# Gated MLP: products accumulated in PSUM chains that ScalarE seeds, two plain pairs a layer, and the first pair's weight blocks made in attention

## The chip, the core and the metric

The kernel runs on one core of one Trainium2 chip. The metric is the device time of one execution in microseconds (us). Engines: TensorE (PE), VectorE (DVE), ScalarE (ACT), GpSimd (POOL) and SyncE (SP), which issues most loads.

## The reference, cut to what matters

A two-layer causal decoder trunk on 512 tokens with 1024 channels, all in float32. Each layer ends with a cross-attention and a gated MLP; the change lies in these two.

```python
def conv_ffn(x, norm, w_up, dw_w, dw_b, w_down):      # d_ff = 3072
    h = rms_norm(x, norm) @ w_up
    g = causal_dwconv(h[..., :D_FF], dw_w, dw_b)       # width 3
    u = h[..., D_FF:]
    return (jax.nn.gelu(g) * u) @ w_down

for layer in range(2):
    x = x + (mixer_ab(x) if layer == 0 else conformer_conv(x))
    x = x + cross_attn(x, mem, ...)                    # 4 heads, 256 memory tokens
    x = x + conv_ffn(x, ...)
return rms_norm(x, final_norm)
```

## The kernel before

Channels lie on the 128 partitions, tokens along the free dimension: an activation is 8 tiles of 128 x 512. Each operand of a matmul is a pair of rounded numbers, `hi` (made by ScalarE as a converting copy) and `lo` (made by VectorE as the difference); one product of a weight block and an activation block takes three matmuls (`mm3`: hi·hi, hi·lo, lo·hi; lines L186, L187, L188).

**Pairs.** The 3072 hidden channels are 24 groups `c` of 128. Each `c` has a gate block and a value block of w_up, together a "pair". The first `PLAIN` = 3 pairs are computed plainly: 8 k-blocks times 3 matmuls of 512 columns for the gate, the same for the value. The other 21 go through a two-by-two scheme with seven half products in place of eight (`Seven`, `Blocks`, `unit`): the weights of a pair are four 512-column blocks, from which sums r, z are formed; the seven left operands are named a11, a12, a22, s1, s2, s3, s4. Right operands are the halves of the normalised input (B11, B21, B22) and four sums of them (T1 to T4, made by `Seven.sums`, once for each k of 0 to 3). Each half product is 12 matmuls of 256 columns.

**Blocks of a pair.** The pair comes in by three loads (`Blocks.load`: r and z; `load_second`: a12 and a22). Each block needs a `high` (ScalarE, L797) and a `low` (VectorE, L804). The sums are formed in place by DMAs that add (GpSimd's queue), each issued behind a `low`: r += z after a11, z += a22 after a22, r += a22 after s3, r += a12 after s2. So s3 is made of r after the first addition, s1 of z after its addition.

**A unit of before** (`unit(c)`) makes the seven products in seven PSUM banks in turn, in the order a11, a12, s2, s3, s1, s4, a22. VectorE adds them together (`add`, L171), ScalarE copies the first home. `gating` then multiplies with the norm's factor `norm.r`, runs the convolution (Identity on ScalarE, two steps on VectorE), gelu (ScalarE), and makes `ys[c]`. Blocks of the next two pairs are converted in between. From c = 4 on, a unit also makes two down outputs of 12 matmuls of 512 columns (`Down.out`, tag `aux`), which VectorE adds to the residual `X` (`Down.sum`).

**Opening.** `opening()` makes the plain pairs (`start(0)` to `start(5)`, gates and values by turns) while the norm's factor is found from the sum of squares (`mean_of`, `scale_of`: a table load, a square root, a reciprocal L308) and while the last of the sums, `seven.sums(3)`, the first pair's blocks and the second pair's first blocks are made. `gate(c)` is the gate's path up to gelu, `values(c)` multiplies and makes the high part, `close(c)` the low part.

**Attention** runs before it: `scores` (products, row maximum L501 to L505, exponentials L510 and normalisation L517 on ScalarE), `transpose` (L531 on TensorE), `turned`, `mixed`, and `back`, the output projection that adds to `X` (L555) and feeds the MLP's norm.

**Order.** Both stages are under `manual_schedule`: on PE, ACT, DVE and POOL the instructions stand in the order in which the code is written, and an engine that waits holds up everything behind. SP's loads wait for a free buffer (the ring `raw` has 3, `wa` has 4).

Of the kernel before, what the change touches and what calls it, by code (L numbers as in the profile page):

```python
# [13 lines left out]
ALU = mybir.AluOpType  # L14
# [13 lines left out]
PLAIN = 3  # L28
# [33 lines left out]
def trunk(ctx: ExitStack, tc: tile.TileContext, I: dict, out: list):  # L62
# [121 lines left out]
    def mm3(ps, w, x, first, last):  # L184
        (wh, wl), (xh, xl) = w, x
        PE.matmul(ps, wh, xh, start=first, stop=False)  # L186
        PE.matmul(ps, wh, xl, start=False, stop=False)  # L187
        PE.matmul(ps, wl, xh, start=False, stop=last)  # L188
# [281 lines left out]
    def attention(layer, norm, mem, nxt, six):  # L470
# [197 lines left out]
        with tc.manual_schedule(engines=ORDERED):  # L668
# [25 lines left out]
            end(3, "a12")  # L694
        back(0, range(4))
# [18 lines left out]
    class Seven:  # L714
# [38 lines left out]
        def product(self, ps, w, j, first=True):  # L753
            for c in range(4):
# [6 lines left out]
                mm3(ps, blk(w, c * P), x, first and c == 0, c == 3)  # L761
# [55 lines left out]
    def ffn(layer, norm, nxt, seven):  # L817
        ys = {}

        class Down:  # L820
# [8 lines left out]
            def out(self, i, ps):  # L829
                for k in range(GC):  # L830
                    mm3(ps, blk(self.w, k * 2 * P + i * P), ys[self.g * GC + k], k == 0, k == GC - 1)
                return lambda: self.sum(i, ps)
# [7 lines left out]
        pairs = {c: Blocks(I["wpair"][layer * (CF - PLAIN) + c - PLAIN]) for c in range(PLAIN, CF)}  # L840
        downs = {c: Down(*divmod(c - GC, GC)) for c in range(GC, CF + GC)}

        early = set()

        def high(c, name):
            if c in pairs and (c, name) not in early:
                pairs[c].high(name)

        def low(c, name):
            if c in pairs and (c, name) not in early:  # L850
                pairs[c].low(name)

        def gating(c, f, g, ps, u3):
# [3 lines left out]
            V.tensor_tensor(g, g, norm.r, op=ALU.mult)  # L857
            A.activation(y, g, AF.Identity, scale=dw(2), bias=col("f_dw_b", layer * CF + c))
            yield
            add(f[:, :M], ps, u3)  # L860
            V.tensor_tensor(f, f, norm.r, op=ALU.mult)
            for s in (1, 2):
                V.scalar_tensor_tensor(y[:, s:], g[:, : T - s], dw(2 - s), y[:, s:], op0=ALU.mult, op1=ALU.add)
            yield
            A.activation(y, y, AF.Gelu_apprx_tanh)
            yield
            V.scalar_tensor_tensor(y, f, -1.0, y, op0=ALU.mult, op1=ALU.mult)
            ys[c] = act_r(), act_r()
# [3 lines left out]

        def unit(c):

# [989 lines left out]
```

## Time and profile before

| | |
|---|---|
| median of 3 runs | 1430.1 us (1429.94 to 1431.17) |
| span of the profiled execution | 1429.2 us |
| the profiled execution's time | not listed apart; its span lies 0.9 us below the median of the runs |
| PE busy | 1418.0 us (99%) |
| DVE busy | 1184.4 us (83%) |
| ACT busy | 800.7 us (56%) |
| POOL busy | 311.2 us (22%) |

The span falls into stages (from the timeline, us): mixer of layer 0 to about 245, attention to 355, the MLP's opening to 388, its 21 units to 709, the last down outputs to 731, the conformer to about 888, attention and MLP of layer 1 from about 935 to 1396, the final norm to the end. A row of a timeline is: start, duration, engine, line, operation, output<-inputs, partitions x elements, count, and in brackets the idle time just ahead with the engine whose work ended it. Matmul rows overlap by pipelining, so the price of a matmul is the distance of starts, not the duration shown.

### The profile page before, as it was taken

The numbers are of one execution on the slowest core, as the hardware profiler recorded it, in microseconds if no ns is written. First come the engines' busy times: TensorE is split into PE (matmuls) and PEld (weight loads), VectorE is DVE, ScalarE is ACT, GpSimd is POOL, SyncE is SP. The second block draws the span as 40 slices with busy tenths as digits, with TensorE's granted clock in tenths as the row PEclk, the third lists the DMA queues.
The fourth block names the chain that finished last, engine by engine and source line by source line (L and its number), as shares of the span: only waits on it lengthen the run. The fifth ranks groups of instructions, "written<-read, shape, count | busy, mean of one in ns | idle before, by whom it ended". The sixth has DMA issues, their size and how long they took to land.

```text
span 1429.2 us, 22885 instructions
## 1 busy us (share of the span) xinstructions
PE 1418.0 (99%) x8578; PEld 1259.4 (88%) x8578; DVE 1184.4 (83%) x1980; ACT 800.7 (56%) x1336; POOL 311.2 (22%) x325
## 2 busy tenths in 40 slices
PE   9999999999999999999999999999999999999998
PEld 7988888998899999999988777899889999999997
DVE  6987776778888888888888997978788988888885
ACT  7678754666644444544555547767665444444434
POOL 0011310200122221222008992010012222221201
PEclk9999999999999999999999999999999999999999
DMA  8523232542577777777432454345247876877741
GB/s 302 197 74 104 89 119 80 118 111 89 136 183 169 172 181 165 164 176 169 140 119 89 118 158 153 105 87 148 86 114 162 178 184 157 171 183 159 164 127 60
DMA packets 78591, 202.23 MB, mean 141 GB/s; under 512 B 8848, under 2 KB 9360, under 8 KB 78480
## 3 DMA queue, kind: packets, MB, share of 16 engines
q1 hardware_dynamic: 50544, 150.15, 33.6%
q0 software_dynamic: 27648, 50.34, 21.3%
q8 instruction: 67, 1.10, 0.3%
q14 instruction: 44, 0.36, 0.1%
q10 hardware_dynamic: 288, 0.27, 0.1%
HBM read 145.16 MB, written 2.10 MB: 103 GB/s over the span
## 4 chain that ended last, share of the span: by engine, by line
PE 90%; DVE 3%; DMA 2%; POOL 2%; issue 1%; ACT 1%; SPq 0%; POOLq 0%; DVEq 0%; ACTq 0%
PE mm L187 22%; PE mm L186 22%; PE mm L188 22%; PE aux L186 7%; PE aux L187 7%; PE aux L188 7%; PE mm L458 2%; DMA raw<-in_wv 1%; DVE wlo L167 1%; POOL actf L1469 1%; ACT whi L166 1%; PE aux L531 0%; POOL act L167 0%; POOL tmp L1290 0%; DMA raw<-in_pw 0%
## 5 line engine op out<-in xcount | busy, mean ns | idle before, releaser
L187 PE MATMUL mm<-act,whi 128*128 128x512 f32 (+2 forms) x1077 | 377.1, 350 | 0.6 <-DVE act L181 0.5
L188 PE MATMUL mm<-act,wlo 128*128 128x512 f32 (+2 forms) x1077 | 376.7, 350 | 0.0
L186 PE MATMUL mm<-act,whi 128*128 128x512 f32 (+2 forms) x1077 | 376.6, 351 | 0.0
L187 PEld LDWEIGHTS mm<-act,whi 128*128 128x128 f32 x1077 | 203.7, 189 | 29.0 <-DVE act L167 1.0
L186 PEld LDWEIGHTS mm<-act,whi 128*128 128x128 f32 x1077 | 203.4, 189 | 28.4 <-ACT tmp L1468 0.8
L188 PEld LDWEIGHTS mm<-act,wlo 128*128 128x128 f32 x1077 | 203.6, 189 | 25.8
L797 ACT ACTIVATE bigr<-raw 128x512 fp32r<-128x512 f32 x168 | 105.6, 628 | 166.8 <-DMA raw<-wa 70.4
L188 PE MATMUL mm<-bigr,bigr 128*128 128x256 f32 x672 | 190.2, 283 | 0.0
L187 PE MATMUL mm<-bigr,bigr 128*128 128x256 f32 x672 | 190.2, 283 | 0.0
L186 PE MATMUL mm<-bigr,bigr 128*128 128x256 f32 x672 | 190.0, 283 | 0.0
L171 DVE TENSOR_TENSOR tmp<-mm,tmp 128x256 f32<-128x256 f32 x336 | 136.3, 419 | 31.6 <-PE mm L188 25.9
L186 PE MATMUL aux<-act,whi 128*128 128x512 f32 x399 | 156.3, 392 | 0.0
L187 PE MATMUL aux<-act,whi 128*128 128x512 f32 x399 | 156.2, 391 | 0.0
L188 PE MATMUL aux<-act,wlo 128*128 128x512 f32 x399 | 155.2, 389 | 0.0
L804 DVE TENSOR_TENSOR bigr<-raw,bigr 128x512 fp32r<-128x512 f32 x168 | 115.5, 688 | 37.0 <-ACT bigr L797 34.8
L166 ACT ACTIVATE whi<-raw 128x1024 fp32r<-128x1024 f32 (+1 forms) x95 | 96.4, 1019 | 84.1 <-PE mm L187 44.0
L187 PEld LDWEIGHTS mm<-bigr,bigr 128*128 128x128 f32 x672 | 128.9, 192 | 1.6
L186 PEld LDWEIGHTS mm<-bigr,bigr 128*128 128x128 f32 x672 | 128.9, 192 | 1.5
L188 PEld LDWEIGHTS mm<-bigr,bigr 128*128 128x128 f32 x672 | 128.9, 192 | 0.0
L807 POOL DMA_DIRECT2D raw<-raw x48 | 41.6, 866 | 343.1 <-DVE wlo L804 283.3
L811 POOL DMA_DIRECT2D raw<-wa x48 | 41.5, 864 | 308.3 <-DVE bigr L804 258.5
L167 DVE TENSOR_TENSOR wlo<-raw,whi 128x1024 fp32r<-128x1024 f32 (+1 forms) x75 | 90.5, 1210 | 20.0 <-ACT whi L166 19.8
(351 smaller groups left out, 3026.1 us busy)
## 6 DMA issues: line engine op xcount, KB each, us to landing
raw<-wa POOLq DMA_DIRECT2D x144, 256.0 KB, 4.6
wa<-in_wpair SPq DMA_DIRECT2D x84, 256.0 KB, 3.5
raw<-in_wpair SPq DMA_DIRECT2D x42, 512.0 KB, 5.7
big<-in_wdown SPq DMA_DIRECT2D x42, 512.0 KB, 6.7
raw<-raw POOLq DMA_DIRECT2D x48, 256.0 KB, 7.6
raw<-in_pw SPq DMA_DIRECT2D x24, 512.0 KB, 3.4
raw<-in_win SPq DMA_DIRECT2D x20, 512.0 KB, 3.4
raw<-in_wk SPq DMA_DIRECT2D x16, 512.0 KB, 3.6
```

What stands on the lines that cost most here:

```text
L166: A.activation(hi, src, AF.Copy)
L167: fetched[1] = (eng or V).tensor_tensor(lo, src, hi.bitcast(F32), op=ALU.subtract)
L171: V.tensor_tensor(out, a, b, op=ALU.add)
L186: PE.matmul(ps, wh, xh, start=first, stop=False)
L187: PE.matmul(ps, wh, xl, start=False, stop=False)
L188: PE.matmul(ps, wl, xh, start=False, stop=last)
L458: PE.matmul(p, m[j], x, start=k == 0 and j == 0 and x is hi, stop=k == C - 1 and x is lo)
L797: A.activation(self.w[name][0], self.block(name), AF.Copy)
L804: V.tensor_tensor(lo, self.block(name), hi.bitcast(F32), op=ALU.subtract)
L807: G.dma_start(self.r, self.z, accum_op=ALU.add)
L811: G.dma_start(self.r, self.a22, accum_op=ALU.add)
L1469: G.tensor_tensor(z[:, s:], z[:, s:], f[:, s:], op=ALU.add)
```

## The change

`PLAIN` goes from 3 to 2, so 22 pairs go through the seven-product scheme, and the first of them is c = 2. A unit's products accumulate in three PSUM chains G, F and H in place of seven banks: a11 starts G; ScalarE copies G into F's bank ("seeds" it, L922), and s2, s3 and a22 add onto F; a12 adds onto G; s1 starts H and s4 adds onto it. ScalarE copies F after s2 (L939) and after s3 (L953) for the parts that VectorE still adds. `ahead(c + 1)` makes the next pair's a11 and the seed inside the unit before. Down outputs start from a bank into which ScalarE copies X (`bank`), are made together behind the chain's s3, and are copied home by ScalarE (`home`) instead of added by VectorE. The loads of the first pair are issued in attention, and `prepare` converts its a11, a22, a12, s3 and s1 there, between the attention's steps. The opening has four plain products, its `seven.sums(3)` stands ahead of `values(0)` and of `gate(1)`, and it converts only s2 of the first pair and a11, a22 of the second.

```diff
-PLAIN = 3
+PLAIN = 2
@@ attention
+        up.load()
+        up.load_second()
         back(0, range(4))
         mixed(2)
         scores(3)
         back(0, range(4, 6))
         back(4, range(6))
+        prepare("a11")
         transpose(3)
         turned(3)
         back(1, range(6))
+        prepare("a22")
         mixed(3)
+        prepare("a12", "s3")
         seven = Seven(nxt)
         for k in range(4):
             for n in (k, k + 4):
                 back(n, range(6 if n in acc else 0, C))
+            if k == 1:
+                prepare("s1")
@@ ffn: down outputs
+            def bank(self, i, seeded):
+                ps = aux_ps()
+                if seeded:
+                    A.activation(ps, X[2 * self.j + i], AF.Copy)
+                return ps
+            def home(self, i, ps, seeded):
+                if seeded:
+                    A.activation(X[2 * self.j + i], ps, AF.Copy)
+                else:
+                    self.sum(i, ps)
@@ unit
+        def ahead(c):
+            G, F = main_ps()[:, :M], main_ps()[:, :M]
+            m(c, G, "a11", seven.B11)
+            A.activation(F, G, AF.Copy)
+            return G, F
         def unit(c):
+            G, F = chains
+            down, seeded = downs.get(c), c > GC
+            H = main_ps()[:, :M]
+            m(c, H, "s1", seven.T1)
+            high(c + 1, "s3")
             next(left, None)
+            low(c + 1, "s3")
+            m(c, F, "s2", seven.T2, False)
+            next(left, None)
+            u, f, g = tmp_f(), tmp_f(), tmp_f()
+            A.activation(u[:, :M], F, AF.Copy)
+            next(left, None)
             high(c + 1, "a22")
+            m(c, G, "a12", seven.B21, False)
             next(left, None)
+            if down:
+                d = [down.bank(i, seeded) for i in range(2)]
+            next(left, None)
             low(c + 1, "a22")
+            times_r(g, G, left_half)
             high(c, "s4")
+            m(c, F, "s3", seven.T3, False)
+            A.activation(u[:, M:], F, AF.Copy)
+            low(c, "s4")
+            add(f[:, right_half], H, u[:, M:])
+            V.tensor_tensor(f[:, right_half], f[:, right_half], norm.r[:, right_half], op=ALU.mult)
             high(c + 2, "a11")
+            low(c + 2, "a11")
             high(c + 1, "a12")
             low(c + 1, "a12")
+            if down:
+                for ks in (range(GC - 1), (GC - 1,)):
+                    for i in range(2):
+                        down.products(i, d[i], seeded, ks)
...
+            high(c + 1, "s1")
+            low(c + 1, "s1")
             high(c + 1, "s2")
             low(c + 1, "s2")
+            if down:
+                down.home(0, d[0], seeded)
+            if c + 1 in pairs:
+                chains = ahead(c + 1)
+            if down:
+                down.home(1, d[1], seeded)
+            m(c, H, "s4", seven.B22, False)
+            m(c, F, "a22", seven.T4, False)
+            left = gating(c, g, f, u, F, H)
             next(left)
@@ opening (as it stands afterwards, from the norm's factor on)
             norm.r = scale_of(mean_of(ss))
             start(1)
             fetch(3)
+            w[-1].low()
             g = gate(0)
             next(g)
+            both(first, "s2")
             next(g)
             next(g)
             pairs[second].load()
             pairs[second].load_second()
             downs[GC].load()
+            t = seven.sums(3)
+            next(t)
+            next(g, None)
             start(2)
+            next(t, None)
             values(0)
+            both(second, "a11")
             close(0)
             start(3)
             g = gate(1)
             next(g)
+            both(second, "a22")
             next(g)
             next(g)
+            pairs[second + 1].load()
             next(g, None)
+            chains = ahead(first)
```

The order that this gives, at three places. Names: `bigr` and `whi` hold high parts, `raw` and `wa` a pair's raw blocks, `mm` a PSUM bank, `act` an activation's parts, `tmp` anything between. First ScalarE at the last attention head of layer 0, with the semaphores that each row waits for; before:

```order
L166 ACTIVATE whi_3285<-raw_3283 128x1024 [waits DMAHW5_49]
L166 ACTIVATE act_3067<-mm_3053 128x512 [waits PE_49]
L166 ACTIVATE act_3071<-mm_3060 128x512 [waits PE_49]
L510 ACTIVATE tmp_3089,sm_3093<-tmp_3089,mx_3088,rq_2251 128x256 [waits DVE_49]
L510 ACTIVATE tmp_3089,sm_3093<-tmp_3089,mx_3088,rq_2251 128x256
```

and now:

```order
L166 ACTIVATE whi_3180<-raw_3178 128x1024 [waits DMAHW5_49]
L166 ACTIVATE act_3073<-mm_3059 128x512 [waits PE_49]
L166 ACTIVATE act_3077<-mm_3066 128x512 [waits PE_49]
L810 ACTIVATE bigr_3230<-raw_3040 128x512 [waits DMASW4_49]
L510 ACTIVATE tmp_3095,sm_3099<-tmp_3095,mx_3094,rq_2251 128x256 [waits DVE_49]
L510 ACTIVATE tmp_3095,sm_3099<-tmp_3095,mx_3094,rq_2251 128x256
```

The high part of the first pair's s3 (L810), which waits for an adding DMA of GpSimd's queue, now stands ahead of the last head's exponentials. Second VectorE in the opening of layer 0, from the end of gate 0; before:

```order
L975 TENSOR_TENSOR tmp_3623<-tmp_3623,r_3589 128x512
L978 TENSOR_TENSOR tmp_3623<-mm_3591,tmp_3623 128x512
L983 TENSOR_TENSOR act_3667<-tmp_3623,act_3666 128x512
L963 TENSOR_TENSOR tmp_3710<-mm_3640,r_3589 128x512
L203 TENSOR_TENSOR wlo_3672<-raw_3669,whi_3671 128x1024
L804 TENSOR_TENSOR bigr_3683<-raw_3530,bigr_3683 128x512
L969 SCALAR_TENSOR_TENSOR tmp_3712<-tmp_3710,par,tmp_3712 128x511
L969 SCALAR_TENSOR_TENSOR tmp_3712<-tmp_3710,par,tmp_3712 128x510
L740 TENSOR_TENSOR tmp_3725<-tmp_3719,tmp_3718 128x256
```

and now:

```order
L759 SCALAR_TENSOR_TENSOR tmp_3653<-tmp_3653,tmp_3649 128x256
L1011 TENSOR_TENSOR tmp_3631<-tmp_3631,r_3596 128x512
L764 TENSOR_TENSOR bigr_3235<-tmp_3652,bigr_3234 128x256
L764 TENSOR_TENSOR bigr_3237<-tmp_3653,bigr_3236 128x256
L764 TENSOR_TENSOR bigr_3239<-tmp_3652,bigr_3238 128x256
L764 TENSOR_TENSOR bigr_3241<-tmp_3653,bigr_3240 128x256
L1014 TENSOR_TENSOR tmp_3631<-mm_3598,tmp_3631 128x512
L817 TENSOR_TENSOR wlo_3697<-raw_3640,whi_3696 128x512
L1019 TENSOR_TENSOR act_3694<-tmp_3631,act_3693 128x512
L1008 TENSOR_TENSOR tmp_3727<-mm_3663,r_3596 128x512
```

Gate 1's first multiply (L963, now L1008) stood ahead of the last sums (L740 on); now it stands behind them (L759 is the last of the four), their low parts (L764), values 0 (L1014), the second pair's a11 (L817) and close 0 (L1019). Third ScalarE from the opening into the first unit; before:

```order
L973 ACTIVATE tmp_3712<-tmp_3712 128x512
L797 ACTIVATE bigr_3768<-raw_3530 128x512
L980 ACTIVATE act_3771<-tmp_3712 128x512
L966 ACTIVATE tmp_3804<-tmp_3802,par 128x512
L797 ACTIVATE bigr_3806<-wa_3677 128x512
L200 ACTIVATE whi_3808<-big_3680 128x1024
L973 ACTIVATE tmp_3804<-tmp_3804 128x512
L797 ACTIVATE bigr_3816<-raw_3674 128x512
```

and now:

```order
L1016 ACTIVATE act_3693<-tmp_3631 128x512
L810 ACTIVATE whi_3696<-raw_3640 128x512
L889 ACTIVATE tmp_3729<-tmp_3727,par 128x512
L810 ACTIVATE bigr_3731<-wa_3643 128x512
L894 ACTIVATE tmp_3729<-tmp_3729 128x512
L922 ACTIVATE mm_3742<-mm_3741 128x256
L810 ACTIVATE bigr_3769<-raw_3640 128x512
```

Gate 1's gelu is L973 on `tmp_3712` before and L894 now; the seed of the first chain F (L922, PSUM to PSUM) stands right behind it.

More of the change, by code (lines that the diff above doesn't have):

```diff
@@ L815, in low, with pairs_of, ffn @@
                 G.dma_start(self.r, self.a12, accum_op=ALU.add)
-    def ffn(layer, norm, nxt, seven):
+    def pairs_of(layer):
+        return {c: Blocks(I["wpair"][layer * (CF - PLAIN) + c - PLAIN]) for c in range(PLAIN, CF)}
+    def ffn(layer, norm, nxt, seven, pairs):
         ys = {}
@@ L988, in opening @@
             w[-1].low()
-            for name in ("a11", "a22", "a12"):
-                high(first, name)
-                low(first, name)
             norm.r = scale_of(mean_of(ss))
@@ L1071, in ffn @@
                 unit(c)
-            due()
             for _ in left:
@@ L1086, in ffn @@
                 for i in range(2):
-                    downs[CF + j].out(i, mm_ps())()
+                    ps = mm_ps()
+                    downs[CF + j].products(i, ps)
+                    downs[CF + j].sum(i, ps)
             return mem, parked
```

174 lines of the change are left out of this document (58 added, 116 removed).

## The prediction

> **What bounds the kernel now.** The profile's page first: busy times, granted clock, and the chain that ended last.
>
> ```profile
> span 1429.2 us, 22885 instructions
> ...
> PE 1418.0 (99%) x8578; PEld 1259.4 (88%) x8578; DVE 1184.4 (83%) x1980; ACT 800.7 (56%) x1336; POOL 311.2 (22%) x325
> ...
> PEclk9999999999999999999999999999999999999999
> ...
> PE 90%; DVE 3%; DMA 2%; POOL 2%; issue 1%; ACT 1%; SPq 0%; POOLq 0%; DVEq 0%; ACTq 0%
> ```
>
> TensorE is busy in 99% of the span at full clock. All idle time together is 11.2 us, so relief for the other engines cannot bring more than that; only fewer or narrower matmuls, or new waits of TensorE, move the end. Next the timeline of TensorE, filtered to the first row of each product, for the price of a matmul in a row of them.
>
> ```profile
> 500.10 0.28 PE L186 MATMUL mm<-bigr,bigr 128*128 128x256 f32 x1
> ...
> 504.41 0.40 PE L186 MATMUL aux<-act,whi 128*128 128x512 f32 x1
> ...
> 507.16 0.28 PE L186 MATMUL mm<-act,whi 128*128 128x256 f32 x1
> ...
> 515.66 0.28 PE L186 MATMUL mm<-bigr,bigr 128*128 128x256 f32 x1
> ```
>
> Three pair products (36 matmuls of 256 columns) take 4.31 us from 500.10, 0.1197 each; a down output (12 of 512) takes 2.75 us from 504.41, 0.229 each. The stretch from 507.16 holds four products and one output: 8.50 by these prices, and 8.50 is shown. The units run without a gap. All times below are of layer 0; layer 1's instructions stand in the same order there, so each term counts twice.
>
> **1. The work removed.** One more pair per layer goes the seven-product way: two plain products (48 matmuls of 512) become 84 of 256. 48 × 0.229 − 84 × 0.1197 = 10.98 − 10.07 = **−0.9 us** a layer. The adds that move from VectorE into PSUM chains relieve VectorE; TensorE is the bound there, so I cost them at nothing.
>
> **2. Blocks made in attention.** Views: timelines of TensorE, ScalarE and VectorE around the last softmax, and the DMA issues of two windows (245 to 316, 355 to 400) with the median time to landing last.
>
> ```profile
> 315.92 1.03 PE L531 MATMUL aux<-ident,tmp 128*128 128x128 f32 x8
> 316.71 0.48 PE L186 MATMUL mm<-act,whi 128*128 128x512 f32 x1
> ...
> 311.70 0.60 ACT L510 ACTIVATE tmp<-tmp,mx,rq 128x256 f32<-128x256 f32 x1 [3.33 <-DVE mx L505]
> ...
> 315.18 0.91 ACT L517 ACTIVATE tmp<-tmp,sm 128x256 f32<-128x256 f32 x2 [0.23 <-DVE sm L515]
> ...
> 306.13 1.22 DVE L167 TENSOR_TENSOR wlo<-raw,whi 128x1024 fp32r<-128x1024 f32 x1
> ...
> 309.60 0.68 DVE L501 TENSOR_TENSOR tmp<-aux,rs 128x512 f32<-128x512 f32 x1
> ...
> 311.51 0.15 DVE L505 TENSOR_TENSOR mx<-mx,rq 128x2 f32<-128x2 f32 x1
> ...
> raw<-raw POOLq DMA_DIRECT2D x2, 256.0 KB, 3.5
> ...
> raw<-raw POOLq DMA_DIRECT2D x3, 256.0 KB, 6.7
> ```
>
> ScalarE's last normalisation ends at 316.09 and TensorE's transposes start at 315.92: just in time, so what delays the exponentials delays TensorE. Now the s3 block's conversion stands on ScalarE directly ahead of these exponentials, and its low part on VectorE ahead of the row maximum that feeds them. s3 exists only after an adding DMA, issued behind a11's low part. VectorE gives that about 306.8 (the place of the 306.13 row, plus a 0.68 instruction). Landing after 3.5 (this stage) to 6.7 us (the opening): high part from 310.3 to 313.5, then high 0.63, low 0.68, maximum 1.3 (the 309.60 row's end at 310.28 to 311.51): exponentials at 313.1 to 316.4 instead of 311.7. Behind the stopped conversion wait both softmax halves, and for them the transposes. That is +1.4 to +4.7. I take **+2.5**, nearer to this stage's own landing, with one us on it since the pair's three loads and both adds now fall together here.
>
> **3. The opening.** TensorE's rows, then ScalarE's, then VectorE's, from the norm's sum to the first unit, and the page's group of the conversions.
>
> ```profile
> 360.48 0.39 PE L287 MATMUL stat<-act,ones 128*128 128x512 f32 x1
> ...
> 360.94 0.40 PE L186 MATMUL mm<-act,whi 128*128 128x512 f32 x1
> ...
> 388.16 0.28 PE L186 MATMUL mm<-act,whi 128*128 128x256 f32 x1
> ...
> 367.59 0.82 ACT L966 ACTIVATE tmp<-tmp,par 128x512 f32<-128x512 f32 x1 [3.33 <-DVE tmp L963]
> ...
> 370.20 1.28 ACT L973 ACT_TABLE_LOAD   x1
> ...
> 376.32 1.32 ACT L734 ACTIVATE tmp<-x,par 128x512 f32<-128x512 f32 x2
> ...
> 379.45 1.37 ACT L748 ACTIVATE bigr<-tmp 128x256 fp32r<-128x256 f32 x4 [1.29 <-DVE tmp L741]
> 380.73 0.62 ACT L973 ACTIVATE tmp<-tmp 128x512 f32<-128x512 f32 x1
> ...
> 363.35 3.35 DVE L308 RECIPROCAL r<-tmp 128x512 f32<-128x512 f32 x1 [0.53 <-ACT tmp L306]
> 366.80 0.69 DVE L963 TENSOR_TENSOR tmp<-mm,r 128x512 f32<-128x512 f32 x1
> 367.41 1.21 DVE L203 TENSOR_TENSOR wlo<-raw,whi 128x1024 fp32r<-128x1024 f32 x1
> 368.54 1.53 DVE L969 SCALAR_TENSOR_TENSOR tmp<-tmp,par,tmp 128x511 f32<-128x511 f32 x2
> ...
> 374.88 0.68 DVE L963 TENSOR_TENSOR tmp<-mm,r 128x512 f32<-128x512 f32 x1
> ...
> 378.67 0.42 DVE L740 TENSOR_TENSOR tmp<-tmp,tmp 128x256 f32<-128x256 f32 x1
> ...
> 380.13 0.68 DVE L804 TENSOR_TENSOR wlo<-raw,whi 128x512 fp32r<-128x512 f32 x1
> 380.74 1.42 DVE L751 TENSOR_TENSOR bigr<-tmp,bigr 128x256 fp32r<-128x256 f32 x4
> ...
> L797 ACT ACTIVATE bigr<-raw 128x512 fp32r<-128x512 f32 x168 | 105.6, 628 | 166.8 <-DMA raw<-wa 70.4
> ```
>
> Before, five plain products (each 24 × 0.229 = 5.49) fill 360.94 to 388.16 while the other engines catch up. Now only three are left behind the norm, then a11 and s1 of the first pair (1.44 each): TensorE comes to s2 at 360.94 + 16.47 + 2.87 = 380.3. s2 adds onto chain F, which ScalarE must seed by a copy of G, and this copy stands behind gate 1's gelu in ScalarE's queue. That gelu ran at 380.73 before, since gate 1's first multiply (374.88) stood ahead of the last sums. Now the sums, their splits and values 0 stand ahead of it. VectorE and ScalarE by turns, at the distances of these rows (the 0.69 of 366.80 is followed after 0.61, the 1.21 of 367.41 after 1.13):
>
> - reciprocal ends 366.7; piece's low part 367.9; gate 0's multiply 368.5; identity 369.4; s2's high and low parts 370.7; two convolution steps 372.1; table load and gelu 374.1
> - two scaled copies 375.4; four sums 377.0; multiply 377.6; the splits of the sums 378.95; values 0 at 379.6
> - high part of it 380.25; second pair's a11 high and low 381.5; close 382.15; gate 1's multiply 382.8; identity 383.6; a22 high and low 384.85; convolution steps 386.35; gelu 387.0; seed copy 387.3
>
> TensorE stands for 387.3 − 380.3 = **+7.0 us**; with every instruction at its full length and nothing overlapped, 7.6; with quicker changes of engine, 6.5. Moving downs' loads and SP's queue costs nothing: the second pair's load goes into a buffer free since 367, a dozen us before its use.
>
> **4. The first units.** Medians of adding DMAs in 355 to 400 (x6) and 400 to 680 (x18, x54), and the page's group of GpSimd's issues of them:
>
> ```profile
> raw<-wa POOLq DMA_DIRECT2D x6, 256.0 KB, 4.3
> ...
> raw<-raw POOLq DMA_DIRECT2D x18, 256.0 KB, 8.0
> ...
> raw<-wa POOLq DMA_DIRECT2D x54, 256.0 KB, 5.2
> ...
> L807 POOL DMA_DIRECT2D raw<-raw x48 | 41.6, 866 | 343.1 <-DVE wlo L804 283.3
> ```
>
> Units without down outputs last 84 × 0.1197 = 10.07 us, others 15.56; there are now two of the short ones. From the seed at 387.3, s3 of pair 2 ends 391.7, and ideally s1 of pair 4 starts 6 + 7 products after the seed, at 406.0. The chain to it: second-half value and a11 of pair 4 by 393.6 on VectorE; its adding DMA lands after 6.7: 400.3; s3 high and low 401.6; a22 low (now behind s3's) 402.3; its DMA lands after 4.3: 406.6; s1 high and low 407.9; two issues on GpSimd at 0.8 each, since a landing counts from some point within its issue: 409.5. **+3.5**. With 3.5 and 3.4 us landings it would be hidden (0); with 8.0 and 5.2 it is +5.7. I take the landings of the opening's own window. In units with down outputs the 5.5 us more cover it.
>
> **5. Layer ends.** The last down outputs keep their number and order, and last values come earlier than they are needed: nothing. The one wait of the old conformer norm:
>
> ```profile
> 735.30 1.05 PE L314 MATMUL stat<-onesf,tmp 128*128 128x1 f32 x8 [0.80 <-DVE tmp L248]
> ```
>
> VectorE, with fewer adds, may be ahead there and save up to 0.8; I leave it at nothing.
>
> **Sum.** −0.9 + 2.5 + 7.0 + 3.5 = +12.1 a layer, +24.2 in all: span 1453.4. The runs' median of 1430.1 lies 0.9 above the span shown, so about **1454**. Low ends: −0.9 + 1.4 + 6.5 + 0 = 7.0, 1444; without any attention wait 1441. High ends: −0.9 + 4.7 + 7.6 + 5.7 = 17.1, 1464.
>
> **Rivals.**
>
> Clock falls in the long wait. The program's start has 20 small matmuls after idling:
>
> ```profile
> 1.03 4.12 PE L139 MATMUL stat<-onesf 128*128 128x128 f32 x20 [1.03 <-POOL onesf L128]
> ```
>
> They take 4.12/20 = 0.206 us each, while eight of that shape take 0.79/8 = 0.10 between 315.92 and 316.71. So a cold TensorE runs at half rate for 4.1 us or more and loses 2.1. If each 7 us wait does this, 4.2 more: 1458. For it: the stall is the first that long; against it: no row shows a clock that fell in a wait. [...]
>
> The other side: no wait appears. If gate 1's chain is done by 380.3 (the seed copy 7 us earlier than my sum, which it is if ScalarE and VectorE overlap where I put them in series) and the landings are the short ones, only −0.9 × 2 is left: 1428.3, within the bound; with the 0.80 at the conformer's norm saved as well, −2.6, and faster by the bound once another 0.3 of the 11.2 idle us goes: 1427. Against it: rows with their order make nearly every step in series.
>
> A wait in every unit. If the adding DMAs land later than about 9.3 us after issue in the steady units, s3 stops ScalarE each time; 0.7 us over 40 units is +28: 1482. The median of 8.0 speaks against it, but is close.
>
> **Chances.** Forecast 0.58; clock falls 0.20; every unit waits 0.06; other slower ways 0.05; no wait, within the bound 0.07; faster 0.04. The range 1441 to 1467 runs from the opening's wait alone to the high ends with part of the clock's loss; it leaves out 0.17 and some of the tails. Measurement tells no change from 0.2%, 2.9 us. Faster 0.04, same 0.07, slower 0.89.
>
> **What would show it.** Right: an idle of TensorE near 380, some 7 us, ended by ScalarE's seed copy; transposes of the last softmax later by 1 to 5 us; idle in the second and third unit; none after, with unit distance 15.56. Wrong: first unit starting by 381, exponentials at 311.7 as before, or TensorE idle in steady units. A granted clock below full in the slice at 390 decides the clock's case.

## The result, and the profile after

The changed kernel takes 1469.35 us (1468.6 to 1472.91, four runs) beside 1430.57 us for the kernel before on the same chip (1429.94 to 1431.17, four runs): ratio 1.0274, 95% interval 1.0259 to 1.0289. It is slower by some 38.8 us. The forecast was 1454 with a range to 1467: the direction and the places were right, the size was not.

The page of the profiled execution (span 1466.9, 13.5 us over the 1453.4 that the sum gave), its lines on busy time, on the chain that ended last, and the group of the pair products' first matmuls, with the idle time ahead of them at the end:

```profile
span 1466.9 us, 22867 instructions
...
PE 1430.8 (98%) x8650; PEld 1270.4 (87%) x8650; DVE 1079.3 (74%) x1796; ACT 905.0 (62%) x1588; POOL 317.7 (22%) x333
...
PE 81%; DVE 6%; DMA 5%; ACT 3%; issue 3%; POOL 2%; SPq 0%; POOLq 0%; ACTq 0%; DVEq 0%
...
L186 PE MATMUL mm<-bigr,bigr 128*128 128x256 f32 x704 | 202.0, 287 | 16.4 <-ACT mm L922 11.9
```

VectorE lost 105 us of work, as meant, and TensorE's share of the chain fell from 90% to 81%. By the page, the seeds (L922) end 11.9 us of TensorE's waits.

Where the time went is told by three marks that both kernels have in each layer: the first head's transposes, the sum for the MLP's norm, and the column sums of the norm that follows the MLP. TensorE's timeline before (the other two marks of layer 0 stand in the prediction: 360.48 and 735.30):

```profile
268.12 1.04 PE L531 MATMUL aux<-ident,tmp 128*128 128x128 f32 x8
...
955.00 1.03 PE L531 MATMUL aux<-ident,tmp 128*128 128x128 f32 x8
...
1047.35 0.39 PE L287 MATMUL stat<-act,ones 128*128 128x512 f32 x1
...
1414.91 0.72 PE L1163 MATMUL stat<-onesf,tmp 128*128 128x1 f32 x6
```

and after:

```profile
268.88 1.04 PE L531 MATMUL aux<-ident,tmp 128*128 128x128 f32 x8
...
368.02 0.39 PE L287 MATMUL stat<-act,ones 128*128 128x512 f32 x1
...
753.86 0.98 PE L314 MATMUL stat<-onesf,tmp 128*128 128x1 f32 x8
...
973.22 1.04 PE L531 MATMUL aux<-ident,tmp 128*128 128x128 f32 x8
...
1072.85 0.49 PE L287 MATMUL stat<-act,ones 128*128 128x512 f32 x1 [0.33 <-ACT act L166]
...
1452.61 0.73 PE L1174 MATMUL stat<-onesf,tmp 128*128 128x1 f32 x6
```

Attention, from the first to the second mark: 92.4 and 92.4 us before (layers 0 and 1), 99.1 and 99.6 after. MLP, from the second to the third: 374.8 and 367.6 before, 385.8 and 379.8 after. So attention gives 6.8 + 7.3 and the MLP 11.0 + 12.2, 37.3 of the span's 37.7. Between 1160 and 1420 us, in layer 1's units, no matmul waits: the steady units keep their pace.

**Attention.** TensorE's rows at the last head, ScalarE's two rows there, and the adding DMA's issue on GpSimd:

```profile
319.31 0.88 PE L531 MATMUL aux<-ident,tmp 128*128 128x128 f32 x2 [2.23 <-ACT tmp L517]
321.04 1.54 PE L531 MATMUL aux<-ident,tmp 128*128 128x128 f32 x6 [0.85 <-ACT tmp L517]
322.24 0.78 PE L186 MATMUL mm<-act,whi 128*128 128x512 f32 x1
...
314.35 0.63 ACT L810 ACTIVATE bigr<-raw 128x512 fp32r<-128x512 f32 x1 [4.98 <-DMA raw<-raw]
...
317.00 0.60 ACT L510 ACTIVATE tmp<-tmp,mx,rq 128x256 f32<-128x256 f32 x1 [2.02 <-DVE mx L505]
...
308.53 0.86 POOL L820 DMA_DIRECT2D raw<-raw  x1 [16.10 <-ACT act L166]
```

ScalarE stands 4.98 us at s3's conversion, until the adding DMA issued at 308.53 has landed (5.8 us later), and the exponentials begin at 317.00. The transposes then come in two parts, with a second wait, and take 2.93 us (319.31 to 322.24) in place of 0.79.

**Opening and first units.** The two waits of TensorE and the ScalarE rows that end them:

```profile
394.43 0.58 PE L186 MATMUL mm<-bigr,bigr 128*128 128x256 f32 x1 [5.96 <-ACT mm L922]
...
416.93 0.39 PE L186 MATMUL mm<-bigr,bigr 128*128 128x256 f32 x1 [1.59 <-ACT bigr L810]
...
393.48 0.63 ACT L894 ACTIVATE tmp<-tmp 128x512 f32<-128x512 f32 x1 [2.27 <-DVE tmp L892]
394.01 0.37 ACT L922 ACTIVATE mm<-mm 128x256 f32<-128x256 f32 x1
...
416.25 1.15 ACT L810 ACTIVATE bigr<-raw 128x512 fp32r<-128x512 f32 x2 [3.29 <-DMA raw<-wa]
```

The seed stands behind gate 1's gelu, and s1 of the third pair behind its adding DMA, as forecast.

**The clock.** Stretches of the profile: window, length, busy time of PE, PEld (TensorE's weight loads), DVE, ACT and POOL with the number of instructions, then the granted clock, DMA share and GB/s. The last three are the 3.41 us up to each fall of the clock in layer 0.

```profile
315.00:330.00 15.00, 11.91 (x44) 9.22 (x43) 4.39 (x10) 5.42 (x15) 1.33 (x2) 0.77 0.27 52
385.00:405.00 20.00, 13.67 (x100) 13.26 (x100) 13.44 (x26) 8.20 (x16) 3.93 (x5) 0.83 0.49 114
405.00:430.00 25.00, 22.97 (x154) 21.46 (x153) 19.03 (x33) 14.03 (x25) 6.44 (x8) 0.93 0.82 174
...
388.00:389.00 1.00, 0.47 (x4) 0.27 (x3) 1.00 (x2) 0.00 (x0) 0.06 (x1) 1.00 0.00 0
...
390.00:391.00 1.00, 0.00 (x0) 0.00 (x0) 0.00 (x0) 1.00 (x2) 0.00 (x0) 0.98 0.99 389
391.00:392.00 1.00, 0.00 (x0) 0.00 (x0) 0.76 (x2) 0.21 (x1) 0.00 (x0) 0.50 1.03 215
397.00:398.00 1.00, 1.00 (x7) 1.00 (x7) 0.01 (x1) 0.61 (x2) 0.38 (x1) 0.61 0.08 14
398.00:399.00 1.00, 1.00 (x11) 1.00 (x10) 0.00 (x0) 0.30 (x1) 0.00 (x0) 1.00 1.12 195
...
315.86:319.28 3.42, 1.22 (x6) 0.68 (x4) 2.09 (x6) 2.27 (x8) 0.86 (x1) 1.00 0.86 153
387.54:390.96 3.42, 0.93 (x8) 0.72 (x7) 1.89 (x3) 1.46 (x3) 0.86 (x1) 1.00 0.43 133
414.85:418.26 3.41, 1.59 (x12) 1.18 (x11) 1.45 (x4) 1.42 (x3) 0.00 (x0) 1.00 0.82 150
```

In layer 0 the clock falls to half at each of the three waits, not at the long one alone: at 319.3 and 391.0 for 6.8 us each and at 418.3, just behind the third wait, for 3.4. In layer 1 it falls at the first two only (1025.8 for 3.4 us, 1097.5 for 6.8). In the opening TensorE stops at about 388.5, the clock falls at 391.0 and comes back at 397.8. A stay at half is 3.41 or 6.83 us here, and layer 0's falls lie whole multiples of 3.41 apart: 71.7 us is 21 of them, 27.3 is 8. In the 3.41 us that end with each fall TensorE was busy for 0.36, 0.27 and 0.47 of the time.

### The profile page after: what moved, and what is told of

It reads as the page before. It is cut to its first block, busy times and chain, and to the rows that moved or that the text cites. A ratio compares the mean times of both kernels' runs of the same rounds, so it can differ in the third digit from the quotient of the medians.

```text
span 1466.9 us, 22867 instructions
## 1 busy us (share of the span) xinstructions
PE 1430.8 (98%) x8650; PEld 1270.4 (87%) x8650; DVE 1079.3 (74%) x1796; ACT 905.0 (62%) x1588; POOL 317.7 (22%) x333
## 4 chain that ended last, share of the span: by engine, by line
PE 81%; DVE 6%; DMA 5%; ACT 3%; issue 3%; POOL 2%; SPq 0%; POOLq 0%; ACTq 0%; DVEq 0%
PE mm L186 19%; PE mm L187 19%; PE mm L188 19%; PE aux L186 7%; PE aux L187 7%; PE aux L188 7%; PE mm L458 2%; DMA raw<-wa 2%; DMA raw<-raw 1%; DMA raw<-in_wv 1%; DVE bigr L817 1%; POOL actf L1480 1%; ACT tmp L510 1%; DVE tmp L892 1%; DVE wlo L167 0%
## 5 line engine op out<-in xcount | busy, mean ns | idle before, releaser
L187 PE MATMUL mm<-act,whi 128*128 128x512 f32 (+2 forms) x1061 | 370.7, 349 | 0.5 <-DVE act L181 0.4
L186 PE MATMUL mm<-act,whi 128*128 128x512 f32 (+2 forms) x1061 | 370.7, 350 | 0.0
L188 PE MATMUL mm<-act,wlo 128*128 128x512 f32 (+2 forms) x1061 | 370.3, 349 | 0.0
L186 PE MATMUL mm<-bigr,bigr 128*128 128x256 f32 x704 | 202.0, 287 | 16.4 <-ACT mm L922 11.9
L188 PE MATMUL mm<-bigr,bigr 128*128 128x256 f32 x704 | 201.1, 286 | 0.4 <-DVE bigr L817 0.4
L187 PE MATMUL mm<-bigr,bigr 128*128 128x256 f32 x704 | 200.9, 285 | 0.0
L810 ACT ACTIVATE bigr<-raw 128x512 fp32r<-128x512 f32 x176 | 105.4, 621 | 109.1 <-DMA raw<-wa 97.2
L817 DVE TENSOR_TENSOR bigr<-raw,bigr 128x512 fp32r<-128x512 f32 x176 | 117.6, 688 | 70.5 <-ACT bigr L810 70.5
L186 PEld LDWEIGHTS mm<-bigr,bigr 128*128 128x128 f32 x704 | 136.8, 194 | 18.0 <-ACT mm L922 12.3
L188 PEld LDWEIGHTS mm<-bigr,bigr 128*128 128x128 f32 x704 | 136.9, 194 | 0.9 <-DVE bigr L817 0.9
L187 PEld LDWEIGHTS mm<-bigr,bigr 128*128 128x128 f32 x704 | 137.0, 195 | 0.0
L171 DVE TENSOR_TENSOR tmp<-mm,tmp 128x256 f32<-128x256 f32 x130 | 53.9, 419 | 65.8 <-PE mm L188 64.1
```

Of the source, the lines that this page charges most:

```text
L171: V.tensor_tensor(out, a, b, op=ALU.add)
L186: PE.matmul(ps, wh, xh, start=first, stop=False, skip_group_check=onto)
L187: PE.matmul(ps, wh, xl, start=False, stop=False, skip_group_check=onto)
L188: PE.matmul(ps, wl, xh, start=False, stop=last, skip_group_check=onto)
L810: A.activation(self.w[name][0], self.block(name), AF.Copy)
L817: V.tensor_tensor(lo, self.block(name), hi.bitcast(F32), op=ALU.subtract)
```

## The experiments

Times are medians; the ratio to the kernel before, measured on the same chip, has its interval beside it. "Attention" and "MLP" are the two stretches above, layer 0 / layer 1, from each kernel's one profile.

| run | us | ratio (95%) | attention | MLP |
|---|---|---|---|---|
| before | 1430.6 to 1432.0 | 1 | 92.4 / 92.4 | 374.8 / 367.6 |
| changed | 1469.4 | 1.0274 (1.0259 to 1.0289) | 99.1 / 99.6 | 385.8 / 379.8 |
| w_all | 1472.8 | 1.0285 (1.0264 to 1.0306) | 99.3 / 101.0 | 389.8 / 383.1 |
| w_att | 1466.5 | 1.0244 (1.0227 to 1.0262) | 97.6 / 96.2 | 386.2 / 378.6 |
| att_back | 1456.3 | 1.0170 (1.0155 to 1.0186) | 93.4 / 93.1 | 386.1 / 380.4 |
| gate_left | 1469.1 | 1.0259 (1.0242 to 1.0276) | 99.8 / 100.3 | 384.7 / 379.9 |
| early4 | 1466.5 | 1.0243 (1.0228 to 1.0259) | 98.7 / 100.1 | 385.2 / 379.5 |
| one_load | 1470.1 | 1.0270 (1.0253 to 1.0287) | 99.4 / 99.8 | 385.7 / 380.1 |
| units_only | 1433.2 | 1.0009 (1.0000 to 1.0018) | 92.4 / 92.4 | 376.4 / 367.8 |
| plain2_old | 1456.5 | 1.0175 (1.0159 to 1.0190) | 92.4 / 92.4 | 386.7 / 381.4 |
| fix_a | 1456.9 | 1.0177 (1.0162 to 1.0193) | 93.2 / 93.0 | 385.0 / 380.6 |
| fix_b | 1451.4 | 1.0136 (1.0121 to 1.0151) | 94.1 / 92.9 | 383.4 / 377.5 |
| fix_b_warm | 1449.9 | 1.0126 (1.0111 to 1.0141) | 92.9 / 92.8 | 383.3 / 376.5 |
| no_adds | 1452.3 | 1.0147 (1.0130 to 1.0164) | 93.6 / 93.0 | 383.8 / 377.1 |
| no_gate1 | 1451.7 | 1.0151 (1.0131 to 1.0172) | 93.8 / 92.9 | 383.8 / 377.8 |
| no_both | 1438.3 | 1.0050 (1.0035 to 1.0065) | 93.5 / 93.1 | 376.4 / 370.6 |
| gate_no_adds | 1444.1 | 1.0091 (1.0076 to 1.0106) | 93.1 / 93.2 | 379.5 / 373.7 |

### Is it the clock? (w_all, w_att)

```diff
+    def warm(n):                      # results are never read
+        ps = stat_ps()
+        for i in range(n):
+            PE.matmul(ps, ones, Wx[0], start=True, stop=True)
...
+        warm(9)      # ahead of transpose(3)
+        warm(24)     # between s1 and s2 of the first pair
+        warm(6)      # ahead of s1 of the third pair
```

> The changed kernel with matmuls that nobody reads put into TensorE's three waits of each layer: 9 of 512 columns (2.1 us) ahead of the last head's transposes, 24 (5.5 us) between s1 and s2 of the first pair, 6 (1.4 us) ahead of s1 of the third pair. They fill the waits and lengthen none. Theory (the miss of 13.5 us in the span is the clock, which falls in each wait and stays at half for 3.4 or 6.8 us): the waits end where they ended, the granted clock stays at 1.00, and of the 13 us lost at half rate 9 to 13 come back: 1456 to 1460. Rival (the slow rows after a wait have another cause, or the waits themselves are mis-sized): 1469, within 2, with the slow rows still there.

The time did not fall. (Its four runs spread from 1469.4 to 1476.5 and the profiled one is the longest, so the table's lengths for it are on the high side.) The opening's stretch of this kernel, TensorE's waits, and the adding DMA and ScalarE row behind the second of them:

```profile
385.00:405.00 20.00, 19.16 (x136) 17.63 (x135) 14.30 (x25) 8.92 (x17) 4.30 (x5) 1.00 0.45 106
...
393.62 0.38 PE L193 MATMUL mm<-bigr,bigr 128*128 128x256 f32 x1 [0.46 <-ACT mm L931]
...
408.71 0.39 PE L193 MATMUL mm<-bigr,bigr 128*128 128x256 f32 x1 [1.87 <-ACT tmp L954]
...
418.70 0.39 PE L193 MATMUL mm<-bigr,bigr 128*128 128x256 f32 x1 [1.69 <-ACT bigr L819]
...
400.44 0.86 POOL L829 DMA_DIRECT2D raw<-raw  x1 [3.87 <-DVE wlo L826]
...
407.24 0.63 ACT L819 ACTIVATE bigr<-raw 128x512 fp32r<-128x512 f32 x1 [3.64 <-DMA raw<-raw]
```

In layer 0's opening and first units the clock stays at 1.00 and the seed comes when it came, but TensorE, now quicker, waits at 408.71 where it did not wait before, and the third pair's s1 starts at 418.70 in place of 416.93. The copy that it waits for stands in ScalarE's queue behind s3 of the third pair, whose adding DMA was issued 2.3 us sooner than in the changed kernel (400.44 for 402.71) and still landed later: ScalarE starts on s3 at 407.24, in the changed kernel at 406.73. In layer 1 the same place has a wait of 3.28 us, and the granted clock of the whole execution is 0.996. In the first units other engines and the adding DMAs set the end, and the half clock was hidden under them. In attention the fill failed (the clock still fell there, behind the second wait: 0.89 from 315 to 330), so that place was tried alone, with both its waits filled:

```diff
+        warm(10)     # ahead of the last head's transposes
+        warm(4)      # between its second and third transpose
```

> The changed kernel with matmuls that nobody reads in attention alone: 10 of 512 columns ahead of the last head's transposes and 4 more between its second and third transpose, so that both waits there (2.2 and 0.9 us) are filled and lengthened by nothing. Theory (in attention the half clock itself costs time, since TensorE alone is behind there): the granted clock stays at 1.00 between 315 and 330, the stretch from the transposes to the norm's sum falls from 45.8 to 43.8 us as in the kernel before, 2.5 to 3 us a layer: 1463 to 1465. Rival (as in the opening, other engines set the end of that stretch too): clock at 1.00 and the time within 2 of 1469.

Its stretch of attention, to be set beside the 0.77 of the changed kernel's:

```profile
315.00:330.00 15.00, 14.87 (x68) 11.49 (x67) 5.12 (x12) 6.44 (x16) 0.86 (x1) 1.00 0.26 52
```

Attention gets shorter by 1.5 and 3.4 us with the clock held. Behind the start of the last head's transposes, where the clock acts, the gain is 1.6 and 2.4 us (47.1 and 45.8 us to the norm's sum, beside 48.7 and 48.1); the other 1.0 us of layer 1 is a shorter wait. The median, 2.9 us lower, lies between the two forecasts, the intervals overlap at their ends, and early4 below, a change elsewhere, falls by as much; the profiled run is also the quickest of its four (1463.2). So it is the stretch in the profile that carries this, not the times. There the half clock does cost, some 2 us a layer: behind the wait no other engine holds TensorE up (in the changed kernel it is busy for all 45.78 us from 322.24 to the norm's sum at 368.02).

### Attention (att_back)

```diff
-        prepare("a12", "s3")
+        prepare("a12")
-            if k == 1:
-                prepare("s1")
@@ opening, ahead of norm.r = scale_of(...)
+            both(first, "s3")
+            both(first, "s1")
```

> The changed kernel with the first pair's s3 and s1 converted in the opening, ahead of the norm's factor, in place of attention (a11, a22, a12 stay in attention). Theory (the s3 conversion ahead of the last exponentials makes the attention's wait, and the wait makes the clock fall): 3.1 us of waits and 3.3 us of half clock a layer go, 13 in all: 1456 to 1458. Rival (the two conversions only move: ScalarE and VectorE are late by 1.3 us or more in the opening, whose wait then grows): 1459 to 1464. Rival (the delay of attention comes from the loads and adds issued there, which stay): above 1466.

1456.3, as the theory said. TensorE's row of the last head of layer 1 there:

```profile
1015.49 1.03 PE L531 MATMUL aux<-ident,tmp 128*128 128x128 f32 x8
```

In layer 1 all eight transposes run at once again (in layer 0 six of them still wait 0.26 us), and attention takes 93.4 and 93.1. s3 and s1 were not moved apart from each other; that s3 makes the wait is read from the rows above. The two conversions cost the opening nothing that shows (386.1 and 380.4, beside 385.8 and 379.8). The other three blocks made in attention, with their loads, still cost 0.7 to 1.0 a layer.

### Units, and the plain pair (units_only, plain2_old)

units_only is the kernel before with only the unit changed (`PLAIN = 3`, old `opening` with `chains = ahead(first)` at its end, no `prepare`).

> The kernel before with the new unit alone: three plain pairs, the old opening (its second pair's blocks and the sums where they were) and the old attention; products in chains, seeds and down outputs as changed, the first pair's a11 and seed behind the last plain product. Theory (steady units cost nothing; the losses lie in the opening and in attention): 1430 to 1434, with at most 1 or 2 us of wait a layer at the first seed. Rival (the new units wait for adding DMAs by themselves, above all the first short one): 1437 or more.

1433.2, ratio 1.0009: under three plain pairs the new unit neither wins nor loses anything that can be told from noise. plain2_old is the opposite: the kernel before with one number changed and the steps that fall away.

```diff
-PLAIN = 3
+PLAIN = 2
@@ opening
-            fetch(4); fetch(5); start(4); start(5); gate(2)
+            # behind gate(1): s2 of the first pair, a22 and s3 of the second, downs[GC].w
-                values(2); close(2)
+                values(1); close(1)
```

> The kernel before with two plain pairs in place of three and nothing else: old units with VectorE's adds, old attention, the opening's steps in their old order with the third pair's left out (the second pair's a22 and s3 and the first pair's s2 come behind gate 1). Theory (the opening's 11 us of plain matmuls were the cover under which the other engines caught up, and no order of theirs replaces it; two short units of 10 us follow, where VectorE has 12.7 us of work): 4 to 9 us lost a layer against 0.9 won, 1437 to 1447. Rival (the chains' order and the seed make the opening's wait): 1428 to 1432.

1456.5, more than expected, and its MLP is the longest of all but one (386.7 and 381.4): with old units, old attention and the old order, taking one plain pair out costs as much as the whole MLP part of the change. So the MLP's loss needs neither the chains nor the seed nor the new order of the opening. The waits are other ones, though, seven in layer 0 and none over 2.5 us; the three longest:

```profile
383.06 0.39 PE L188 MATMUL mm<-bigr,bigr 128*128 128x256 f32 x1 [1.00 <-DVE bigr L804]
...
387.69 0.39 PE L186 MATMUL mm<-bigr,bigr 128*128 128x256 f32 x1 [1.73 <-DVE tmp L978]
...
416.09 0.80 PE L186 MATMUL aux<-act,whi 128*128 128x512 f32 x1 [2.47 <-ACT act L869]
```

They end by a low part, by a step of the plain pairs' values (L978) and by the first unit's result (L869). That the two kernels lose nearly the same is shown; that they lose it on the same path is not.

### Moving one thing in the opening (gate_left, early4, one_load, fix_a, fix_b, fix_b_warm)

```diff
+            chains = ahead(first)          # gate_left: ahead of start(3)
             start(3)
-            g = gate(1) ...
+            left = rest()                  # gate(1), values(1), close(1) inside the first unit
+            next(left)
```

> The changed kernel with the first pair's a11 and its seed copy made ahead of the fourth plain product, and gate 1 and values 1 made step by step inside the first unit, where other units make the gating of the unit before. Theory (the opening's wait is ScalarE's queue order alone, the seed copy behind gate 1's gelu): the wait of 6 us shrinks to 1 or less, no clock falls there, 2 x (5 + 1.7) = 13 us less: 1454 to 1458. Rival (the wait only moves to s3 of the first pair, whose bank the copy behind gate 1's steps must free): half of it at most, 1462 to 1466.

Nothing came back (1469.1). The wait at the seed is gone, and these stand in its place:

```profile
393.96 0.51 PE L186 MATMUL mm<-bigr,bigr 128*128 128x256 f32 x1 [2.55 <-ACT tmp L939]
...
407.12 0.38 PE L186 MATMUL mm<-bigr,bigr 128*128 128x256 f32 x1 [1.32 <-ACT tmp L939]
...
415.95 0.39 PE L186 MATMUL mm<-bigr,bigr 128*128 128x256 f32 x1 [1.90 <-ACT bigr L810]
```

early4 converts the third pair's a11 at the end of the opening and its a22 a unit sooner, and issues that pair's second loads in the opening (which the diff here leaves out):

```diff
             chains = ahead(first)
+            both(second + 1, "a11")
@@ unit
-            high(c + 1, "a22")   ...   low(c + 1, "a22")
+            high(c + 2 if c == first else c + 1, "a22")   ...   low(the same)
```

> The changed kernel with the third pair's a11 converted at the end of the opening, its a22 one unit sooner, and its second loads issued in the opening. Theory (what sets the first units is a chain through that pair: a11's low part, adding DMA, s3, a22, adding DMA, s1; it runs beside TensorE and decides when s1 of the third pair starts): the waits of 2 to 2.5 us a layer between 404 and 420 go, with the 1.7 us of half clock behind them: 1460 to 1463. Rival (the first units are set by the opening's lateness and the loads, and the chain only looks critical): 1467 to 1470.

The wait at s1 of the third pair went and a wait of 1.70 us one pair later came. The MLP stays within 0.6 of where it was. The median is 2.9 us lower, between the two forecasts; the profiled run, the longest of its four, does not show where. one_load drops a load that the changed kernel issues twice (44 of the down weights' loads in place of 42):

```diff
-            if c + 2 in downs and c + 2 <= CF:
+            if c + 2 in downs and GC < c + 2 <= CF:
```

> The changed kernel without a load that it issues twice: the first down weights (512 KB) are loaded in the opening and again in the first unit, since that unit's rule loads those of two pairs on. Theory (the adding DMAs of the first units land late because loads crowd them): up to 1 us a layer, 1467 to 1469. Rival: no change, within 1 of 1469.

No change. fix_a is att_back with early4, fix_b adds gate_left:

> Both undone: s3 and s1 of the first pair out of attention, and the third pair's a11 and a22 sooner; the opening's order stays. If the parts add: 1456.3 less 6 to 8, 1448 to 1450. If the third pair's chain is not what sets the first units: 1456.

> As the kernel with both undone, and besides the seed copy ahead of the fourth plain product and gate 1 inside the first unit. By itself that reorder saved nothing, which I read so: the third pair's chain set the end anyway. Theory: with that chain gone the reorder pays 3 to 4 us of the 6 us wait and 1.7 of the clock a layer: 1438 to 1442. Rival (the reorder only moves the wait to the copy behind gate 1's gelu, as long): the same as with both undone, within 2.

fix_a gave what att_back alone gave. fix_b gave 5.5 us more, about half of the 9 to 11 forecast for the reorder, and its 1451.4 lies far above the 1438 to 1442 forecast for both. With its waits filled (14 matmuls ahead of s3 of the first pair, 5 ahead of s3 of the third):

> The kernel with s3 and s1 out of attention, the third pair's blocks sooner and gate 1 inside the first unit, and besides matmuls that nobody reads in its two waits of each MLP: 14 of 512 columns ahead of s3 of the first pair (a wait of 3.7 us), 5 ahead of s3 of the third (1.3 us). Theory (half clock costs time wherever TensorE alone is behind, and here the third pair's chain is out of the way): 2 to 3.5 us a layer, 1444 to 1447. Rival (the first units are set by the other engines and the DMAs, the half clock is hidden under them as in the kernel with all waits filled): 1450 to 1452.

1449.9 beside 1451.4, intervals overlapping; the clock is at 1.00 from 385 to 430 us of layer 0, and at 0.999 over the whole execution. In the MLP the clock is not the loss, to within the 1.5 us between the two.

### Two paths side by side (no_adds, no_gate1, no_both, gate_no_adds)

All four stand on att_back. no_adds and no_gate1 leave out the work that their diffs show, no_both leaves out both, and gate_no_adds is no_adds with gate_left's order.

```diff
+        for c in range(PLAIN + 1, PLAIN + 4):      # no_adds
+            pairs[c].plain = True                  # low() returns ahead of its adding DMA
@@ gate                                             # no_gate1
+                if c == 1:
+                    y[c] = g                       # no convolution, no gelu, no second multiply
```

> The kernel with s3 and s1 converted in the opening (1456.3), with the adding DMAs of the second to fourth pair (c = 3, 4, 5) left out, so that their sums are not made and nothing waits for them. Theory A (the opening's serial chain through gate 1 sets the first units): 1454 to 1457. Theory B (the adding DMAs of those pairs set them): 1448 to 1452. Theory C (each of the two alone is covered by the other): 1454 to 1457, and both together well below.

> The same kernel (1456.3) with its adding DMAs, and without gate 1's convolution, gelu and second multiply, some 4.5 us of ScalarE and VectorE by turns. Theory A: the seed copy comes 4.5 us sooner and all behind it, with 1.7 us of half clock: 1444 to 1448. Theory B or C: 1453 to 1457.

> The same kernel (1456.3) without the adding DMAs of c = 3, 4, 5 and without gate 1's chain. Theory A: as without gate 1 alone. Theory B: as without the adds alone. Theory C: 1438 to 1446, more than the two single savings together.

> The same kernel (1456.3) without the adding DMAs of c = 3, 4, 5, and with the seed copy ahead of the fourth plain product and gate 1 inside the first unit. The reorder alone saved nothing where the adds stood. Theory B or C (it was the adds that took its gain): 1446 to 1450, at least 4 below the kernel without adds alone. Theory A (it only moves the wait): within 2 of the kernel without adds alone.

Alone, the adds give 4.0 us and gate 1's chain 4.6; together 18.0, more than twice their sum. att_back ran on another chip; by the ratios it is 3.3, 2.7 and 17.2. The intervals of the two single kernels overlap that of att_back, so what each gives alone is not settled; that both together give far more is. The reorder gave 0.3 to the changed kernel and gives 8.2 here, with the adds gone; but these stand on different attention, and between them fix_b had 5.5 with the adds in place, so this pair is weaker evidence. Theories A and B, by which both together give no more than one, fail. Theory C holds, though each single saving is some 2 us above what it allowed (1452.3 and 1451.7 for 1454 to 1457): two paths end at nearly the same time, and each hides the other. The second path is seen where the first is cut, in ScalarE's queue of no_gate1, with TensorE's row that it releases:

```profile
382.44 0.36 ACT L920 ACTIVATE mm<-mm 128x256 f32<-128x256 f32 x1
387.55 0.63 ACT L808 ACTIVATE bigr<-raw 128x512 fp32r<-128x512 f32 x1 [4.74 <-DMA raw<-raw]
...
388.60 0.36 ACT L937 ACTIVATE tmp<-mm 128x256 f32<-128x256 f32 x1
...
389.02 0.38 PE L186 MATMUL mm<-bigr,bigr 128*128 128x256 f32 x1 [3.02 <-ACT tmp L937]
```

The seed now comes at 382.44, but ScalarE then stands 4.74 us at the second pair's s3, which waits for its adding DMA, and the copy that frees F for s3 of the first pair stands behind it.

## Why the prediction was wrong, by its steps

**The work removed (-0.9).** Not measured by itself; the steady stretch runs without waits, which fits.

**Attention (+2.5, measured 6.8 and 7.3).** This is the step that failed: the term was mis-sized, and with 9.1 us for both layers it is the largest part of the 13.5. The mechanism was right, and the wait that was priced came within its span of 1.4 to 4.7: the last head's transposes start 50.4 and 51.5 us after the first head's, in place of 47.8, which is +2.6 and +3.7. (That +2.6 meets the 2.5 taken is in part luck: counted from the first head, the exponentials came 4.5 us late, near the high end, and the transposes made up some of it.) What the term left out is all behind that point: it stopped at the first transposes, and the clock was considered for the opening's wait alone. The softmax's second half is late as well (0.85 and about 1 us more), and TensorE then runs at half clock, in layer 0 through the transposes and some 4 us of products. From the start of the transposes to the norm's sum that is 4.1 and 3.6 us, of which holding the clock returned 1.6 and 2.4.

**Opening (+7.0, measured 5.96 at the place and by the releaser named, and 0.37 ahead of s1, ended by VectorE).** The chain of steps came out within a microsecond: shifted by the 7.5 us by which this layer's norm sum is later, the seed was due at 394.8 and ended at 394.4. What was wrong is what the text made of it, that queue order makes this wait. Gate_left removes the order, plain2_old never had it, and both lose nearly the same. So the term's size was near the measured one although what it named was not the only path. The plain pair was 11 us of TensorE work under which a fixed amount of other work was done, on two paths.

**First units (+3.5, measured 1.59 and 0.22).** The third pair's s1 waits at the place named (the second number is for its low part). Its start came out: due at 409.5, with the shift 417.0, measured 416.93. The wait is shorter because TensorE came later itself, some 1.6 us of it by the half clock behind the seed (15 matmuls in 3.37 us from 394.43, which at 0.1197 each are 1.80). But early4 shows that this chain is one of several. Sum for the MLP: forecast -0.9 + 7.0 + 3.5 = 9.6, measured 11.0 and 12.2, which is 4.0 us of the miss.

**Layer ends (0).** Nearly right: the 0.80 us wait ahead of the conformer's norm, left as a possible saving, is gone from the row at 753.86, and from there to layer 1's first transposes it is 219.4 us, before 219.7.

**The clock's rival** was given one fall of 2.1 us a layer, 1458. It happened three times in layer 0 and twice in layer 1, and after shorter waits than the 7 us named. Yet only attention's fall counts for much, since the MLP's is hidden. The stays at half clock are 3.41 or 6.83 us, beside the 4.1 or more taken from the start's rows. The length of a wait alone does not tell which one costs the clock: it fell some 2.5 us after the last matmul in the opening, and in the first units 1.3 us after the end of a wait of 1.59 us, with TensorE busy for 0.27 and 0.47 of the 3.41 us before. It did not fall at the same wait of layer 1 (1.45 us, ahead of 1122.72), nor after the 1.87 us in w_all.

**The other side** (no waits: 1428.3) failed where the text said, at serial steps.

Open ends: no_both still takes 376.4 and 370.6 in the MLP, 2.5 and 3.9 over what the matmul count alone would give (374.8 and 367.6 less 0.9). That stays open. Nor is each fall's price in attention split from the second wait. No version tried here beats the kernel before; units_only is level with it.

## What to carry to other kernels

Work of the busiest engine may be cover for a pipeline that is filling: before taking it out of a stage's opening, add up what the other engines and DMAs must finish under it, not only what the removed work costs. Where several paths end together, cutting one may show little (4.0 and 4.6 us here, 18.0 for both); cut two at once before calling either harmless. And price a new wait on TensorE with what follows it: the second half of the late work, and the clock (together 4.1 and 3.6 us in attention here, of which holding the clock returned 1.6 and 2.4).

## What the runs showed of the hardware

The granted clock fell after TensorE had stood for about 2.5 us (388.5 to 391.0), in the opening's wait that lasted 6 us, and stayed at half for 6.8 us. The five falls in the two layers of the changed kernel (319.28, 390.96, 418.26, 1025.84 and 1097.52) lie 21, 8, 178 and 21 times 3.41 us apart, and in the 3.41 us ahead of them TensorE was busy for 0.36, 0.27, 0.47, 0.19 and 0.00 of the time. At half clock the starts of its matmuls lay 0.213 us apart with 256 columns (394.81 to 397.58) and 0.427 with 512 (322.81 to 325.80), in place of 0.1197 and 0.229. Filling waits with matmuls that nobody reads held the clock at 1.00 in w_all from 385 to 430 us, in w_att from 315 to 330 and in fix_b_warm from 385 to 430, and brought time back only in attention (1.6 and 2.4 us).

One adding DMA of 256 KB that was issued sooner did not land sooner: 6.8 us after its issue at 400.44 in w_all, 4.0 us after 402.71 in the changed kernel, by the ScalarE rows that waited for it.
